# Layer 0 window attention: score matmuls of the two key groups issued in turns

## The chip, the cores and the metric

The kernel runs on 1 core of one Trainium2 chip, as one program. The metric is device time in microseconds (us). All numbers come from runs on the chip and from one profiled execution of the program before the change.

## What is computed

The reference is a two-layer trunk over 1024 tokens of 1024 features. Layer 0 runs two head groups side by side, windowed softmax attention with sinks and retention; layer 1 is a gated short convolution. Each layer then attends to 256 memory tokens, with norms before every part and plain residual sums. Only the windowed attention is touched here. Its 8 query heads share 2 key heads of 64 features, and the tokens are cut into 16 chunks of 64:

```python
g = A_Q_HEADS // A_KV_HEADS                       # 4 query heads for each key head
qc = q.reshape(b, n, CHUNK, A_KV_HEADS, g, d)     # CHUNK = 64, d = 64
kb, vb = band(k), band(v)                         # this chunk's and the two before: 192 keys
scores = jnp.einsum('bnqhgd,bnkhd->bnhgqk', qc, kb) * (d ** -0.5)
m = jnp.maximum(jnp.max(scores, axis=-1, keepdims=True), sink_logit)
p = jnp.exp(scores - m)
denom = jnp.sum(p, axis=-1, keepdims=True) + jnp.exp(sink_logit - m)
out = jnp.einsum('bnhgqk,bnkhd->bnqhgd', p / denom, vb)
```

## The kernel before

Every product of float32 values is made of three passes on TensorE: each operand is cut into a high and a low part, and `mm3` (lines 125 to 130) adds high x high (L128), high x low (L129) and low x high (L130) into one PSUM tile. Each matmul loads its stationary operand first; the profile shows these loads as PEld. The projections (`dense`) go into PSUM tiles named psd, 24 matmuls of 512 columns for each half of the tokens.

`even_layer` (line 409) makes the projections of keys, values and queries, then calls `window_chunk` for the 16 chunks; after every second chunk it calls `dense` for one of the eight gate projections. `window_chunk` does the following for chunk n. Keys lie with features on the partitions, the first key head in rows 0 to 63 and the second in rows 64 to 127, and so do the queries.

- The chunk's queries are split into qh and ql (ScalarE and VectorE, `split`, L144 and L145).
- Scores, in two groups g: rows 0 to 63 of the queries and keys, then rows 64 to 127. Each group takes a PSUM tile (pssc, a bank; two banks in all have this tag) and runs two `mm3`, one for each pair of query heads (jp): 64 rows deep, 128 queries, up to 192 keys. That is 6 matmuls for a group and 12 for a chunk. After each group VectorE reduces its tile to the maxima (mx, L283).
- nm and es (L287, L288), four exponentials on ScalarE (L290) that read the two pssc tiles, the sum, its reciprocal and four scalings on VectorE (L294 to L297) give the probabilities Pe (even chunks) or Po (odd chunks).
- TensorE transposes the probabilities (L311, tiles psa, 4 or 8 of 128 columns), they are split into Th and Tl, and two or four `mm3` multiply them with the values (psa). The results go back in place of the queries (Q, L324).

The order in which instructions stand on an engine is not that of the source. The program is scheduled when it is built: a scheduler with its own timing model takes ready instructions of all chunks and projections and writes one fixed order for each engine, with semaphore waits between engines. On TensorE the score matmuls of a chunk so stand among projection matmuls, value products and the transposes of an earlier chunk, in one stretch or in pieces.

The letters A and B below stand for the score matmuls of the first key group (rows 0 to 63) and of the second (rows 64 to 127); a run is a row of score matmuls on TensorE with no other matmul between them.

Of the kernel before, what the change touches and what calls it, by code (L numbers as in the profile page):

```python
# [19 lines left out]
PSUM = bass.MemoryType.PSUM  # L20
DRAM = bass.MemoryType.DRAM

P = 128
# [16 lines left out]
class Weights:  # L40
    """Streams [128, 1024] weight tiles: load, then an exact split into two float32r parts."""

# [35 lines left out]
class Trunk:  # L78
# [27 lines left out]

    # tiles: each tag is one stream of buffers
    BUFS = {"xh": 8, "xl": 8, "r": 8, "e": 4, "T": 5, "v": 4, "t": 5, "k": 4}
# [14 lines left out]

    # products
    def mm3(self, o, ah, al, bh, bl, first, last):
        """o += a.T @ b for a = ah + al, b = bh + bl, in three float32r passes."""
        mm = self.nc.tensor.matmul
        mm(o, ah, bh, start=first, stop=False)  # L128
        mm(o, ah, bl, start=False, stop=False)  # L129
        mm(o, al, bh, start=False, stop=last)  # L130

    def dense(self, xs, done, parts=((0, H), (H, S)), tags="d"):
        """One 128-feature tile of a projection, for each part of the tokens."""
        wh, wl = self.w.take()
        for i, (a, b) in enumerate(parts):
            ps = self.ps(tags if tags == "d" else tags[i])[:, : b - a]
            for kt in range(KT):
                c = slice(kt * P, kt * P + P)
                xh, xl = xs[kt]
                self.mm3(ps, wh[:, c], wl[:, c], xh[:, a:b], xl[:, a:b], kt == 0, kt == KT - 1)  # L140
            done(a, b, ps)
# [5 lines left out]
    def split_k(self, src, gain=None, two=False):  # L147
        """A [128, 1024] contraction tile's parts, times a gain."""
        nc = self.nc
        hi, lo = self.buf("xh", "xh", dt=F32R), self.buf("xl", "xl", dt=F32R)  # L150
        if gain is None:
            self.split(hi, lo, src)
        else:
            g = self.gains[:, gain : gain + 1]
            for c in halves(two):
                self.last_hi = nc.scalar.activation(hi[:, c], src[:, c], AF.Identity, scale=g)
                nc.vector.scalar_tensor_tensor(lo[:, c], src[:, c], g, hi[:, c].bitcast(F32),  # L157
                                               ALU.mult, ALU.subtract)
        return hi, lo

    def rsqrt(self, var, out=None):
        """(var + EPS) ** -0.5: exp(-ln/2), then a Newton step."""
        nc = self.nc
        n = var.shape[-1]
        r, t = self.buf("t", "rs", (P, n)), self.buf("t", "rt", (P, n))
        out = r if out is None else out
        nc.scalar.activation(r, var, AF.Ln, bias=self.eps)
        nc.scalar.activation(r, r, AF.Exp, scale=-0.5)
        self.last_act = nc.scalar.activation(t, r, AF.Square)
        nc.vector.scalar_tensor_tensor(t, var, EPS, t, ALU.add, ALU.mult)  # L170
        nc.vector.tensor_scalar(t, t, -0.5, 1.5, ALU.mult, ALU.add)
        nc.vector.tensor_tensor(out, t, r, op=ALU.mult)
        return out

    def use_set(self, name):
        """Load a set of activation functions, here in the Activation engine's program."""
        self.tc.keep_in_program_order(self.nc.scalar.preload_act_table_set(name))

    # norms
    def squares(self, m, x, sq, a, b, eng=None):  # L180
        """Square in place of sq, and add to the other features' sums."""
        nc = self.nc
        if m == 0:
            nc.scalar.activation(self.ssq[:, a:b], x, AF.Square)
        else:
            nc.scalar.activation(sq, x, AF.Square)  # L186
            if eng is not None:
                eng.tensor_tensor(self.ssq[:, a:b], self.ssq[:, a:b], sq, op=ALU.add)  # L188

    def mean(self, ones, sq):  # L190
        """The mean of [128, n] squares over the partitions, in each partition."""
        n = sq.shape[-1]
# [6 lines left out]
    def norm(self, rest):  # L199
        """R from the sums of squares and the rest's squares."""  # L200
        for c in (slice(0, H), slice(H, S)):
# [3 lines left out]
    def norm_soon(self, a, b, rest):  # L205
        """The same for tokens a to b, for when the tensor engine waits for it."""
        ps = self.ps("a")[:, : b - a]
# [4 lines left out]
    def scaled(self, out):  # L212
        """Evacuation that applies the tokens' norms; out: columns -> where to."""
        return lambda a, b, ps: self.nc.vector.tensor_tensor(out(a, b), ps, self.R[:, a:b],  # L214
                                                             op=ALU.mult)

    def out_proj(self, ys, x_old, x_new, between=iter(())):
        """x + y @ w, kept on chip and stored, and its squares."""
        nc = self.nc
# [17 lines left out]
    def last_proj(self, ys, x_old, parts):  # L237
        """x + y @ w and the last norm, one part of the tokens after the other."""
        nc = self.nc
# [19 lines left out]

    # layer 0: windowed attention with sinks  # L260
    def window_chunk(self, n, Q, Kh, Kl, V, Pt):
# [12 lines left out]
        mx, nm, sm, es = (self.small(k) for k in ("mx", "nm", "sm", "es"))  # L274
        sc = []
        for g in range(2):
            ps = self.ps("sc")
            r = slice(64 * g, 64 * g + 64)
            for jp in range(2):
                j = slice(jp * P, jp * P + P)  # L280
                self.mm3(ps[:, jp * 256 : jp * 256 + nk], qh[r, j], ql[r, j],
                         Kh[r, k0 : k0 + nk], Kl[r, k0 : k0 + nk], True, True)
            nc.vector.tensor_reduce(mx[:, 2 * g : 2 * g + 2],  # L283
                                    ps.rearrange("p (a b) -> p a b", a=2)[:, :, :nk],
                                    AX.X, ALU.max)
            sc.append(ps)
        nc.vector.scalar_tensor_tensor(nm, mx, -0.125, self.nsink, ALU.mult, ALU.min)  # L287
# [38 lines left out]
    def to_tokens(self, vt, name):  # L326
        """[128 features, tokens] -> [128 tokens, 8 x 128 features], split."""
        hi = self.buf("v", name + "h", dt=F32R)
# [9 lines left out]

    # layer 0: retention
    def rotated(self, t, cos, sin):  # L340
        """Rotary embedding in place, and its parts."""
        nc = self.nc
# [10 lines left out]
    def decayed_q(self, q, dec):  # L353
        """The second half's queries, decayed since the first half's end, split."""
        f, d = self.buf("t", "qd", (P, H)), self.buf("v", "qd", (P, 2, H), F32R)
# [4 lines left out]
    def decayed_k(self, k, h):  # L360
        """The first half's keys by token, decayed to the half's end, split."""
        nc = self.nc
# [45 lines left out]
    def even_layer(self, xs):  # L408
        """Both head groups; returns the output projection's contraction tiles and layer 0's
        memory keys and values."""  # L410
        nc, io = self.nc, self.io
# [64 lines left out]

    # layer 1: gated convolution
    def conv_in(self, xs, kv):
# [34 lines left out]

    # cross-attention
    def mem_norm(self):
        """The normed memory's split contraction tiles for both layers, kept in DRAM."""
        nc = self.nc
# [35 lines left out]
    def mem_k(self, mem):  # L553
        """Keys [features, keys] of the memory, split; one feature tile at each step."""
        K = [self.buf("e", "K", (P, KT, M), F32R) for _ in range(2)]
# [10 lines left out]
    def mem_v(self, mem):  # L566
        """Values [keys, features] of the memory, split; a quarter of the contraction for half
        of the features at each step."""
        V = [self.buf("e", "V", (P, 2, D), F32R) for _ in range(2)]
# [18 lines left out]
    def cross_unit(self, head, half, q, K, V, out):  # L588
        """Attention of one head's 512 tokens; out(dt, columns, PSUM) takes the values."""
        nc = self.nc  # L590
# [41 lines left out]
    def cross(self, xs, K, V):  # L632
        """The heads' values, as contraction tiles; those of all but the last head wait in place
        of the queries until the projections are done."""
        ys, wait = [], []
# [77 lines left out]
def _tiles(w):  # L713
    """[1024, n] -> [n / 128, 128, 8 * 128]: per feature tile, contiguous lines for each partition."""
    n = w.shape[1]
# [27 lines left out]
def _heads(w):  # L743
    """The last 512 columns' heads, as four tiles of [head j | head 4 + j]."""
    return w.reshape(w.shape[0], 2, 4, 64).transpose(0, 2, 1, 3).reshape(w.shape[0], 512)
# [65 lines left out]
```

## Time and profile before

| What | Value |
|---|---|
| time, median of 3 runs | 1514.37 us (1514.28 to 1515.32) |
| span of the profiled execution, first to last instruction | 1513.2 us |
| TensorE busy (matmuls) | 1483.5 us, 98% of the span, 7410 instructions |
| VectorE, ScalarE, GpSimd busy | 769.1, 564.8, 230.3 us |
| window attention with the gate projections | 78 to 226 us of the span |
| score matmuls in it | 192 of 849 matmuls |

The median lies 1.2 us above the span of the profiled execution; what a change does to the span is taken over to the median with that distance. Matmuls are pipelined: a matmul of 512 columns has a duration of 0.39 us in the trace while the next one starts 0.23 us later, so the distance between starts tells what one costs, and a row "x2" in the timeline merges neighbours of one kind.

### The profile page before, as it was taken

To read this page: it belongs to the slowest core of one execution; us is meant where nothing else is said; L and a number is where in the kernel's file an instruction comes from. 1 tells how busy PE (TensorE), PEld (TensorE's weight loads), DVE (VectorE), ACT (ScalarE), POOL (GpSimd) and SP (SyncE) were. 2 spreads that over 40 slices of the span, in tenths; PEclk is the share of its full clock that TensorE was granted. 3 is DMA by queue.
4 is the path that set the end of the run, shared out by engine and by line. 5 is a ranking of instruction groups with operands and counts; after the bars stand their busy time and mean duration, and the time that the engine had idled before them with its cause. 6 is when DMAs were issued, how large, how long until landed. Compare 5 with 4: busy or idle time off the path is not lost.

```text
span 1513.2 us, 18550 instructions
## 1 busy us (share of the span) xinstructions
PE 1483.5 (98%) x7410; PEld 1256.1 (83%) x7410; DVE 769.1 (51%) x1143; ACT 564.8 (37%) x983; POOL 230.3 (15%) x157
## 2 busy tenths in 40 slices
PE   8999999999999999999999999999999999999996
PEld 6878888888788888888888888888888888888996
DVE  7656765556673356444354333332336336446555
ACT  6434652433463244343243111211115225334554
POOL 2300103233401210000211111111110120000233
PEclk9999999999999999999999999999999999999998
DMA  5410104121464521002522221111123532111464
GB/s 212 165 44 29 56 29 139 58 82 43 139 209 153 167 82 44 29 29 70 193 81 102 63 63 56 56 56 56 42 84 113 180 127 74 36 30 40 133 206 151
DMA packets 44421, 140.77 MB, mean 93 GB/s; under 512 B 5552, under 2 KB 11824, under 8 KB 44080
## 3 DMA queue, kind: packets, MB, share of 16 engines
q1 hardware_dynamic: 44336, 139.60, 28.3%
q8 instruction: 58, 0.95, 0.3%
q14 instruction: 27, 0.22, 0.0%
HBM read 112.32 MB, written 23.07 MB: 89 GB/s over the span
## 4 chain that ended last, share of the span: by engine, by line
PE 85%; DVE 5%; DMA 4%; POOL 2%; ACT 1%; issue 1%; SPq 1%; DVEq 0%; POOLq 0%; ACTq 0%
PE psd L130 23%; PE psd L128 23%; PE psd L129 23%; PE pssc L130 3%; PE pssc L129 3%; PE pssc L128 3%; PE psa L128 2%; PE psa L129 2%; PE psa L130 2%; PE psa L311 1%; DMA swap<-bk 1%; DMA swap<-bq 1%; PE psa L621 1%; POOL bk L346 1%; POOL bq L346 1%
## 5 line engine op out<-in xcount | busy, mean ns | idle before, releaser
L128 PE MATMUL psd<-xh,whi 128*128 128x512 f32 (+2 forms) x1736 | 662.0, 384 | 8.4 <-ACT whi L64 7.3
L129 PE MATMUL psd<-xl,whi 128*128 128x512 f32 (+2 forms) x1736 | 663.9, 383 | 0.0
L130 PE MATMUL psd<-xh,wlo 128*128 128x512 f32 (+2 forms) x1736 | 663.1, 383 | 0.0
L128 PEld LDWEIGHTS psd<-xh,whi 128*128 128x128 f32 x1736 | 326.2, 188 | 69.5 <-ACT whi L64 7.8
L129 PEld LDWEIGHTS psd<-xl,whi 128*128 128x128 f32 x1736 | 326.3, 188 | 59.5 <-DVE xl L157 0.3
L130 PEld LDWEIGHTS psd<-xh,wlo 128*128 128x128 f32 x1736 | 326.2, 188 | 59.5
L64 ACT CAST whi<-wraw 128x1024 fp32r<-128x1024 f32 (+1 forms) x155 | 162.0, 1046 | 428.1 <-PE psd L129 306.7
L65 DVE TENSOR_TENSOR wlo<-wraw,whi 128x1024 fp32r<-128x1024 f32 (+1 forms) x155 | 200.6, 1295 | 68.0 <-ACT whi L64 66.1
L188 POOL TENSOR_TENSOR ssq<-ssq,xold 128x512 f32<-128x512 f32 (+2 forms) x54 | 78.1, 1446 | 573.6 <-ACT xold L186 484.3
L227 DVE TENSOR_TENSOR xnew<-psd,xold 128x512 f32<-128x512 f32 x48 | 32.9, 690 | 147.2 <-PE psd L130 143.8
L186 ACT ACTIVATE xold<-xnew 128x512 f32<-128x512 f32 (+2 forms) x63 | 36.4, 580 | 89.2 <-DVE xnew L227 48.9
L144 ACT CAST Th<-psa 128x512 fp32r<-128x512 f32 (+1 forms) x62 | 34.2, 588 | 68.9 <-PE psa L311 36.8
L145 DVE TENSOR_TENSOR Tl<-psa,Th 128x512 fp32r<-128x512 f32 (+1 forms) x62 | 42.1, 686 | 28.3 <-ACT Th L144 28.3
L488 POOL TENSOR_TENSOR y<-y,R 128x512 f32<-128x512 f32 x16 | 24.2, 1514 | 185.4 <-ACT y L487 185.4
L214 DVE TENSOR_TENSOR q<-psd,R 128x512 f32<-128x512 f32 x32 | 22.1, 691 | 53.9 <-PE psd L130 53.8
L611 ACT ACTIVATE P<-pssc,mx 128x256 f32<-128x256 f32 x64 | 29.5, 473 | 43.2 <-DVE mx L609 43.2
L214 DVE TENSOR_TENSOR z<-psd,R 128x512 f32<-128x512 f32 x16 | 11.1, 692 | 61.5 <-PE psd L130 61.5
L495 POOL TENSOR_TENSOR z<-z,R 128x512 f32<-128x512 f32 x16 | 20.7, 1295 | 132.6 <-DVE z L214 132.6
L491 DVE TENSOR_TENSOR y<-psd,y 128x512 f32<-128x512 f32 x16 | 11.0, 690 | 56.9 <-PE psd L130 56.9
L128 PE MATMUL psd<-mn,whi 128*128 128x256 f32 x128 | 36.8, 290 | 2.9 <-DVE K L145 2.9
L130 PE MATMUL psd<-mn,wlo 128*128 128x256 f32 x128 | 37.1, 290 | 0.8 <-DVE wlo L65 0.8
L498 DVE TENSOR_TENSOR z<-psd,z 128x512 f32<-128x512 f32 x16 | 11.1, 691 | 52.2 <-PE psd L130 52.2
(234 smaller groups left out, 1875.5 us busy)
## 6 DMA issues: line engine op xcount, KB each, us to landing
wraw<-w_o SPq DMA_DIRECT2D x32, 512.0 KB, 3.8
wraw<-w_o_in SPq DMA_DIRECT2D x32, 512.0 KB, 3.6
wraw<-w_e_in SPq DMA_DIRECT2D x25, 512.0 KB, 3.7
xold<-x SPq DMA_DIRECT2D x24, 512.0 KB, 4.7
x<-xnew SPq DMA_DIRECT2D x24, 512.0 KB, 2.6
wraw<-w_k SPq DMA_DIRECT2D x16, 512.0 KB, 3.8
wraw<-w_v SPq DMA_DIRECT2D x16, 512.0 KB, 3.6
wraw<-w_q SPq DMA_DIRECT2D x16, 512.0 KB, 3.6
```

Of the source, the lines that this page charges most:

```text
L64: self.nc.scalar.copy(hi[:, c], raw[:, c])
L65: self.nc.vector.tensor_tensor(lo[:, c], raw[:, c], hi[:, c].bitcast(F32), op=ALU.subtract)
L128: mm(o, ah, bh, start=first, stop=False)
L129: mm(o, ah, bl, start=False, stop=False)
L130: mm(o, al, bh, start=False, stop=last)
L144: self.nc.scalar.copy(hi, src)
L145: (eng or self.nc.vector).tensor_tensor(lo, src, hi.bitcast(F32), op=ALU.subtract)
L186: nc.scalar.activation(sq, x, AF.Square)
L188: eng.tensor_tensor(self.ssq[:, a:b], self.ssq[:, a:b], sq, op=ALU.add)
L214: return lambda a, b, ps: self.nc.vector.tensor_tensor(out(a, b), ps, self.R[:, a:b], op=ALU.mult)
L227: nc.vector.tensor_tensor(new[:, a:b], ps, old[:, a:b], op=ALU.add)
L346: nc.gpsimd.tensor_tensor(t, t, cos, op=ALU.mult)
```

## The change

In `window_chunk` both PSUM tiles are taken first. Then for each pair of query heads and each of the three passes the matmul of group 0 is followed by the matmul of group 1, and both reductions to the maxima come after all 12. The matmuls, their operands, their tiles and every other instruction are the same in kind and number. The diff also drops the docstrings and some comments of the file, which changes no instruction; source lines from 287 on stand one line later.

```diff
         mx, nm, sm, es = (self.small(k) for k in ("mx", "nm", "sm", "es"))
-        sc = []
-        for g in range(2):
-            ps = self.ps("sc")
-            r = slice(64 * g, 64 * g + 64)
-            for jp in range(2):
-                j = slice(jp * P, jp * P + P)
-                self.mm3(ps[:, jp * 256 : jp * 256 + nk], qh[r, j], ql[r, j],
-                         Kh[r, k0 : k0 + nk], Kl[r, k0 : k0 + nk], True, True)
+        sc = [self.ps("sc") for _ in range(2)]
+        rows = (slice(0, 64), slice(64, P))
+        keys = slice(k0, k0 + nk)
+        for jp in range(2):
+            j = slice(jp * P, jp * P + P)
+            for i, (a, b) in enumerate(((qh, Kh), (qh, Kl), (ql, Kh))):
+                for g, r in enumerate(rows):
+                    nc.tensor.matmul(sc[g][:, jp * 256 : jp * 256 + nk], a[r, j], b[r, keys],
+                                     start=i == 0, stop=i == 2)
+        for g, ps in enumerate(sc):
             nc.vector.tensor_reduce(mx[:, 2 * g : 2 * g + 2],
                                     ps.rearrange("p (a b) -> p a b", a=2)[:, :, :nk],
                                     AX.X, ALU.max)
-            sc.append(ps)
```

The scheduler writes another order from it, within the window stage alone: before the first score matmul and after the last chunk every engine's order is as it was. Chunk 9 on TensorE, before the change (pssc_1511 is A, pssc_1519 is B; the psa rows with ident are the transposes of chunk 8, psd is a gate projection):

```order
L128 MATMUL pssc_1511<-Kh_361,qh_1503 128x192
L311 MATMUL psa_1474<-ident,Pe_674 128x128 x4
L311 MATMUL psa_1481<-ident,Pe_674 128x128 x4
L129 MATMUL pssc_1511<-Kl_362,qh_1503 128x192
L130 MATMUL pssc_1511<-Kh_361,ql_1504 128x192
L128 MATMUL pssc_1511<-Kh_361,qh_1503 128x192
L129 MATMUL pssc_1511<-Kl_362,qh_1503 128x192
L130 MATMUL pssc_1511<-Kh_361,ql_1504 128x192
L128 MATMUL pssc_1519<-Kh_361,qh_1503 128x192
L129 MATMUL pssc_1519<-Kl_362,qh_1503 128x192
L130 MATMUL pssc_1519<-Kh_361,ql_1504 128x192
```

The same place after the change (pssc_1511 is A, pssc_1512 is B):

```order
L312 MATMUL psa_1474<-ident,Pe_674 128x128 x4
L312 MATMUL psa_1481<-ident,Pe_674 128x128 x4
L282 MATMUL pssc_1511<-Kh_361,qh_1503 128x192
L282 MATMUL pssc_1512<-Kh_361,qh_1503 128x192
L282 MATMUL pssc_1511<-Kl_362,qh_1503 128x192
L282 MATMUL pssc_1512<-Kl_362,qh_1503 128x192
L282 MATMUL pssc_1511<-Kh_361,ql_1504 128x192
L282 MATMUL pssc_1512<-Kh_361,ql_1504 128x192
L282 MATMUL pssc_1511<-Kh_361,qh_1503 128x192
L282 MATMUL pssc_1512<-Kh_361,qh_1503 128x192
L282 MATMUL pssc_1511<-Kl_362,qh_1503 128x192
L282 MATMUL pssc_1512<-Kl_362,qh_1503 128x192
```

The transposes, which stood behind the first A and cut the chunk's scores into runs of 1 and 11, now stand ahead of one run of 12, with A and B in turns.

Not every chunk stands so. Chunk 6 on TensorE after the change (pssc_1249 is A, pssc_1250 is B; psa with Th or Tl are value products of chunk 4):

```order
L282 MATMUL pssc_1249<-Kh_361,qh_1241 128x192
L282 MATMUL pssc_1249<-Kl_362,qh_1241 128x192
L282 MATMUL pssc_1249<-Kh_361,ql_1242 128x192
L128 MATMUL psa_1100<-Th_1084,Vh_424 128x256
L282 MATMUL pssc_1249<-Kh_361,qh_1241 128x192
L282 MATMUL pssc_1249<-Kl_362,qh_1241 128x192
L282 MATMUL pssc_1249<-Kh_361,ql_1242 128x192
L129 MATMUL psa_1100<-Tl_1085,Vh_424 128x256
L130 MATMUL psa_1100<-Th_1084,Vl_425 128x256
L128 MATMUL psa_1100<-Th_1084,Vh_424 128x256
L282 MATMUL pssc_1250<-Kh_361,qh_1241 128x192
L129 MATMUL psa_1100<-Tl_1085,Vh_424 128x256
```

Here value products went between the score matmuls, A and B do not stand in turns, and the chunk has four runs where it had three (AAAAAABBBB, B and B, with transposes between them).

Over the whole stage the program before has 36 runs: 20 with a transpose behind them and 16 with a projection matmul. The program after has 26 runs: 11 with a transpose behind them, 12 with a projection matmul and 3 with a value product. By chunk the runs are, with a comma between two runs of a chunk:

| chunk | before | after |
|---|---|---|
| 0 | AAAAAABBBBBB | ABABABABABAB |
| 1 | AAAAAAB, BBBBB | AAABBBAB, ABAB |
| 2 | AAAAAABB, B, BBB | AAAABBBBA, BAB |
| 3 | AAAAAABB, BBBB | AAAABBBBABAB |
| 4 | AAAAAABBBB, BB | ABABABABABAB |
| 5 | AA, AAAABBBBBB | AAAABBBBABAB |
| 6 | AAAAAABBBB, B, B | AAA, AAA, B, BBBBB |
| 7 | AA, AAAABBBBBB | AABBABABA, BAB |
| 8 | AAAAAABBBB, BB | AABBABABABAB |
| 9 | A, AAAAABBBBBB | ABABABABABAB |
| 10 | AAAAAABBBB, B, B | AAABBBABABA, B |
| 11 | AA, AAAABBBBBB | ABA, BABABABAB |
| 12 | AAAAAABBBB, B, B | AAABBBABABAB |
| 13 | AA, AAAABBBBBB | ABA, BABABABAB |
| 14 | AAAAAABBBB, B, B | AAABBBABABAB |
| 15 | A, AAAAABBBBBB | ABABA, BABABAB |

## Rows read from the trace of the kernel before

**Rows 1.** The page of the profile: the span, the busy time of four engines (share of the span, instructions), and the shares of the chain of work that ended last.

```profile
span 1513.2 us, 18550 instructions
PE 1483.5 (98%) x7410; PEld 1256.1 (83%) x7410; DVE 769.1 (51%) x1143; ACT 564.8 (37%) x983; POOL 230.3 (15%) x157
...
PE 85%; DVE 5%; DMA 4%; POOL 2%; ACT 1%; issue 1%; SPq 1%; DVEq 0%; POOLq 0%; ACTq 0%
```

**Rows 2.** Busy time of each engine by stretches of the span (number of instructions in brackets), then the granted TensorE clock as a share of 2.4 GHz, the share of the DMA engines and GB/s: the window stage, and four stretches behind it.

```profile
78.00:226.00 148.00, 148.00 (x849) 121.57 (x849) 93.52 (x248) 76.29 (x209) 4.60 (x1) 1.00 0.11 36
...
402.00:406.00 4.00, 1.49 (x9) 0.94 (x7) 2.88 (x3) 1.19 (x2) 2.31 (x2) 1.00 0.17 36
406.00:410.00 4.00, 3.89 (x15) 3.03 (x14) 4.00 (x7) 3.57 (x8) 0.06 (x1) 0.57 0.81 246
410.00:440.00 30.00, 26.89 (x207) 25.88 (x206) 23.39 (x32) 18.66 (x31) 7.64 (x6) 1.00 0.71 243
440.00:444.00 4.00, 3.62 (x17) 3.63 (x18) 3.51 (x7) 2.56 (x5) 0.00 (x0) 0.57 0.47 136
```

**Rows 3.** The chain of work that ended last, from 78 to 226 us, by line: shares of those 148 us.

```profile
by line: PE psd L129 20.9%; PE psd L128 20.8%; PE psd L130 20.7%; PE psa L311 10.3%; PE pssc L130 5.0%; PE pssc L128 5.0%; PE pssc L129 4.7%; PE psa L128 4.3%; PE psa L129 4.3%; PE psa L130 4.1%
```

**Rows 4.** TensorE's matmuls in order of time, chunk 8: start in us, duration in us, line, output and inputs, rows*columns of the array in use, moving operand.

```profile
152.27 0.35 PE L128 MATMUL pssc<-Kh,qh 64*128 64x192 f32 x1
152.46 0.27 PE L129 MATMUL pssc<-Kl,qh 64*128 64x192 f32 x1
152.57 0.27 PE L130 MATMUL pssc<-Kh,ql 64*128 64x192 f32 x1
152.58 0.38 PE L128 MATMUL pssc<-Kh,qh 64*128 64x192 f32 x2
152.78 0.29 PE L129 MATMUL pssc<-Kl,qh 64*128 64x192 f32 x2
152.89 0.29 PE L130 MATMUL pssc<-Kh,ql 64*128 64x192 f32 x2
153.00 0.27 PE L128 MATMUL pssc<-Kh,qh 64*128 64x192 f32 x1
```

**Rows 5.** The same view for the stationary loads of that run.

```profile
152.38 0.19 PEld L129 LDWEIGHTS pssc<-Kl,qh 64*128 64x128 f32 x1
152.49 0.19 PEld L130 LDWEIGHTS pssc<-Kh,ql 64*128 64x128 f32 x1
152.58 0.20 PEld L128 LDWEIGHTS pssc<-Kh,qh 64*128 64x128 f32 x2
152.69 0.21 PEld L129 LDWEIGHTS pssc<-Kl,qh 64*128 64x128 f32 x2
```

**Rows 6.** The chain of work that ended last, in order of time (start in us, us that the chain spent there): single score matmuls of chunk 10 among transposes and ahead of a projection.

```profile
172.45 0.81 PE psa L311 x6
173.25 0.28 PE pssc L129
173.54 0.37 PE psa L311 x2
173.90 0.28 PE pssc L130
174.19 0.43 PE psd L129
174.62 0.24 PE psd L130
```

**Rows 7.** The same view for the second run of chunk 5, AAAABBBBBB, with eight transposes ahead of it and a projection behind it.

```profile
125.00 1.02 PE psa L311 x8
126.03 0.28 PE pssc L130
126.31 0.11 PE pssc L128 x2
...
126.77 0.11 PE pssc L130
126.88 0.43 PE psd L129
```

**Rows 8.** The timelines of VectorE (the four scalings of the probabilities of a chunk) and of TensorE (the first transposes of the same chunk): chunk 9 (Po), then chunk 10 (Pe).

```profile
171.30 1.01 DVE L297 TENSOR_SCALAR Po<-Po,sm 128x192 f32<-128x192 f32 x4
...
172.38 0.66 PE L311 MATMUL psa<-ident,Po 128*128 128x128 f32 x4
...
180.62 1.01 DVE L297 TENSOR_SCALAR Pe<-Pe,sm 128x192 f32<-128x192 f32 x4
...
182.11 1.09 PE L311 MATMUL psa<-ident,Pe 128*128 128x128 f32 x8
```

**Rows 9.** TensorE's timeline in the last of those stretches: the first and the last of 14 matmuls of 256 columns, and two behind them.

```profile
440.75 0.41 PE L128 MATMUL psd<-mn,whi 128*128 128x256 f32 x1
...
443.53 0.40 PE L129 MATMUL psd<-mn,whi 128*128 128x256 f32 x1
443.74 0.31 PE L130 MATMUL psd<-mn,wlo 128*128 128x256 f32 x1
443.88 0.28 PE L128 MATMUL psd<-mn,whi 128*128 128x256 f32 x1
444.00 0.28 PE L129 MATMUL psd<-mn,whi 128*128 128x256 f32 x1
```

## Prediction

> **What bounds the kernel now.** I read the page first: TensorE is busy for 1483.5 of 1513.2 us, and 85% of the chain that ended last is its own [rows 1]. So a change helps if TensorE's own stream gets shorter, or if it waits less. Next I took the stage that the change touches. From 78 to 226 us TensorE is busy for all of the 148 us, the clock is granted at 1.00 (2.4 GHz), VectorE is busy for 93.52 us and ScalarE for 76.29 [rows 2]. The chain of this stage holds nothing but TensorE's lines: 14.7% of it is the score matmuls (three rows pssc, 5.0 + 5.0 + 4.7), or 21.8 us [rows 3]. The stage is bound by what TensorE's matmuls cost one after another, so I price the scores in that currency, distance between starts.
>
> **How a run of score matmuls is priced.** The timeline of chunk 8 shows three things [rows 4]. Within A the starts are 0.11 us apart (152.46, 152.57), which is also the distance of the loads of the stationary operand, 152.38 to 152.49 [rows 5]: a key group takes a matmul each 0.11 us, and I call that a slot. Second, A and B do run side by side already: at 152.58 two matmuls L128 are merged, the first B, 0.01 us behind the third A, and the fourth A at 152.69; from there on two matmuls and two loads come in each slot [rows 4, 5]. The first B stands four places behind the third A in the order, so a matmul can start once the one four places ahead has started. Third, work with other shapes costs extra. The first score matmul of a run takes 0.28 us of the chain where a further one takes 0.11 [rows 6, 7], so 0.17 for the way in. On the way out two transposes take 0.37 and eight 1.02 [rows 6, 7]; the difference of six is 0.65, or 0.108 each, so two are worth 0.22 and 0.15 is extra. A projection takes 0.43 instead of 0.24, so 0.20 with rounding [rows 6]. Each run thus has a fixed cost of 0.32 us with a transpose behind it, 0.37 with a projection, and 0.11 for each slot.
>
> Check on before: 20 x 0.32 + 16 x 0.37 = 12.3 us fixed. Slots by the rule: AAAAAABBBB is 6.8 (B begins 2.8 slots in), AAAABBBBBB is 6.2 (126.03 to 126.88 is 0.85 us, less 0.28 that is 5.2 slots behind the first, [rows 7]), a lone group its own number. Over the table of runs: 8.8 + 11 + 10 + 10 for chunks 0 to 3, 8.8 for each of the eight with AAAAAABBBB or A, AAAAABBBBBB, 8.2 for the four with AA, AAAABBBBBB: 143, times 0.11 is 15.7. Together 28.0 us. From the chain: 21.8 on the scores, and on the matmuls behind the runs 20 x 0.15 + 16 x 0.20 = 6.2, again 28.0.
>
> **The change part by part.** *Turns.* With A and B in turns each slot holds one of both from the start, so ABABABABABAB takes 6 slots. The scheduler does not give that everywhere; by the same rule the chunks 0 to 15 after take 6, 4+2, 5+2, 6.2, 6, 6.2, 3+3+1+5, 5+2, 6, 6, 6+1, 2+5, 6, 2+5, 6, 3+4: 108 slots. 143 - 108 = 35 slots, 3.8 us less. The bounds of this term: nothing at all, if A and B in turns run no better than the queue already lets them, and 47 slots or 5.2 us, if all 192 went in pairs (143 - 96).
>
> *Fewer runs.* 26 runs in place of 36, 11 with a transpose behind, 12 with a projection, 3 with a value product. The last kind has no row before; it lies between 0.32 and 0.37, and I take 0.37 since its stationary operand is loaded as a projection's is. 11 x 0.32 + 15 x 0.37 = 9.1 us, 3.2 less than 12.3. This follows from the order alone and doesn't depend on pairs.
>
> *What else moves.* The number of matmuls, of DMAs and of all other instructions is the same, and nothing moves outside the stage, so SP's and GpSimd's queues see the same rows. Both reductions now come behind the twelfth matmul, where the first was done under B's matmuls. What hides that is the distance from the scalings to the transposes of the chunk: in chunk 9, the narrowest, the scalings end at 172.31 and TensorE starts the transposes at 172.38; in chunk 10, the next, they end at 181.63 and the transposes start at 182.11 [rows 8]. In chunk 9 0.07 us is left, and I count 0.1 us of waiting for it; in the others 0.5 us or more covers the later reduction, and it costs nothing. Both PSUM banks must be free when a chunk's scores begin, where A's alone had to be; the exponentials that free them end before the scalings do, so this wait is the smaller one, and I count nothing. Bounds of the two: 0, and 1.6 us if each of the 16 chunks lost 0.1.
>
> Sum: 3.8 + 3.2 - 0.1 = 6.9 us of TensorE's stream. The stages behind it start that much earlier; they are driven by TensorE's own progress and keep their length. Span 1506.3, and with the distance of 1.2 us between span and median, 1507.5 us.
>
> A rule of the Trainium skill says otherwise on the pairs. The rows show B's first matmul running beside A's third and ahead of A's fourth to sixth, which stand earlier in the order [rows 4]. TensorE: Matmul & The Clock Gate, section Part 3: Packing small matmuls, says that matmuls start and end strictly in program order. By that rule before would hold 192 slots and the 36 runs would cost 12.3 + 21.1 = 33.4 us, where the chain shows 28.0; the turns would then save up to 10.6 us instead of 3.8. The trace does not agree, and I go by the rows.
>
> **The rivals.** *The supply is too slow.* No row shows more than two matmuls a slot over four slots, and there only one place of the order had to be brought in for each slot, since A and B were drawn from two places of it. With full turns two have to be. If TensorE's sequencer brings one matmul with its load in 0.11 us, five are at hand at the start and a run of n takes n - 4 slots: 8 in place of 6 for a run of twelve, and over the nine runs of eleven or twelve 17 slots or 1.8 us more: 1509.3 us. Chance 0.14. (The Trainium skill, TensorE: Matmul & The Clock Gate, section Wait — 56ns, not 53.3ns?, gives about 62 ns for each matmul where firmware decodes it; by it twelve matmuls need 0.74 us and not 0.66, an estimate of 0.7 us over the nine runs, so 1508.2 us. No run here shows which decoding is at work.)
>
> *Turns bring nothing, only the fewer runs do.* Then 3.2 us remain, 1514.4 - 3.1 = 1511.3. Against it stands that a B in its own bank beside an A is seen in the rows [rows 4, 7]. This is also the case in which the change does not do what it says. Chance 0.05.
>
> *New waits.* TensorE comes to transposes or scores earlier than VectorE and ScalarE deliver, because the order of these two engines changed as well. For it: 0.07 us of cover in chunk 9 [rows 8]. Against it: the two are busy 63% and 52% of the stage [rows 2]. With 0.2 us in each chunk 3.2 us are lost: 1510.6. Chance 0.07.
>
> *Slower: each change of key group exposes its load.* At the head of a run the second A starts 0.19 us behind the first [rows 4]. If every change between A and B cost that, 192 x 0.19 = 36.5 us, with the fixed 9.1 us 45.6 instead of 28.0: 1532 us. It decides from 0.098 us a matmul on, (28.0 - 9.1) / 192, where the rows show 0.055 with A and B alternating for four slots. Chance 0.05.
>
> *Strict order.* If A and B did not overlap before and do after, the turns would be worth up to 96 x 0.11 = 10.6 us, with the fewer runs 13.8: 1500.6 us. The check of 28.0 us speaks against it. Chance 0.01. (It is what the page's rule on program order would give.)
>
> **How the numbers follow.** The forecast, within about 1 us, has 0.68. Predicted 1507.5. Besides the cases, the clock adds a spread of its own: behind the stage it is granted at 0.57 on average in two stretches of 4 us, 406 to 410 and 440 to 444, each behind a stretch in which TensorE had stood idle for 2.5 us or more [rows 2]; one of them gone or one more is about 1.3 us by the second, where 14 matmuls started 0.21 us apart and the next ones 0.12 [rows 9]. With the slow supply below and the better bound of the turns above, 1505.5 to 1510.8 leaves out the cases at 1511.3 and 1532, part of the waits and the strict order: some 0.15. A measurement of this kernel can tell about 0.2%, 3.0 us, from no change. Faster by more than that: forecast, slow supply, strict order, most of the waits and half of the case at 1511.3, 0.88. Within: 0.07. Slower: 0.05.
>
> **What would show it.** In the profile after: score rows as x2 pairs from the head of a run, starts 0.11 us apart for a pair; the stage from 78 us ending near 219 in place of 226; the chain of the stage with about 10% for the scores; no idle time of TensorE in it. Starts of 0.19 us within a run would show the exposed load, gaps ahead of L312 the late probabilities, pairs that fall apart after the second slot the slow supply. Wrong altogether would be the pricing, if the stage got shorter by 7 us while the score runs kept their lengths.

## The result and the profile after

The changed kernel takes 1507.99 us (median of four runs, 1506.56 to 1509.92) beside 1514.84 us of the kernel before (1514.28 to 1518.75, four runs). The ratio is 0.9948, with a 95% interval of 0.9932 to 0.9964 (5.5 to 10.3 us): 6.9 us less at the median, where 6.9 were forecast. A second comparison (the last experiment below) gives 0.9966, 0.9953 to 0.9978.

The page of the kernel after, the lines that answer to [rows 1]: TensorE's busy time fell by 7.0 us and the span by 6.4.

```profile
span 1506.8 us, 18553 instructions
...
PE 1476.5 (98%) x7410; PEld 1251.4 (83%) x7410; DVE 769.5 (51%) x1143; ACT 564.3 (37%) x983; POOL 230.4 (15%) x157
...
PE 87%; DVE 4%; DMA 4%; POOL 2%; ACT 1%; issue 1%; SPq 0%; DVEq 0%; POOLq 0%; ACTq 0%
```

Windows of the kernel after: the stage, and two stretches behind it (columns as in [rows 2]).

```profile
78.00:219.00 141.00, 140.95 (x849) 116.88 (x848) 93.23 (x248) 74.50 (x202) 4.62 (x1) 1.00 0.12 39
396.00:400.00 4.00, 1.08 (x5) 0.56 (x3) 2.33 (x2) 0.62 (x1) 3.24 (x2) 1.00 0.00 0
400.00:404.00 4.00, 3.53 (x15) 3.37 (x16) 4.00 (x7) 3.61 (x8) 0.00 (x0) 0.57 0.84 249
```

As many matmuls, 849, as filled 148 us now fill 141, and TensorE is idle for 0.05 us of them. The chain of the stage, by line, answers to [rows 3]: the scores (now one line, L282) are 11.6% of 141 us, 16.4 us, where they were 21.8. The prediction said about 10%; its own prices (26 times 0.17 for the way in and 108 slots) make 16.3 us.

```profile
by line: PE psd L128 22.0%; PE psd L130 21.5%; PE psd L129 21.4%; PE pssc L282 11.6%; PE psa L312 9.8%; PE psa L129 4.8%; PE psa L128 4.6%; PE psa L130 4.4%; issue 0.0%
```

How it looks in one run, to be set beside [rows 4]: TensorE's timeline of the kernel after, eleven score matmuls of chunk 10 (AAABBBABABA) between a projection and the transposes of chunk 9.

```profile
167.84 0.40 PE L130 MATMUL psd<-xh,wlo 128*128 128x512 f32 x1
168.17 0.36 PE L282 MATMUL pssc<-Kh,qh 64*128 64x192 f32 x2
168.36 0.28 PE L282 MATMUL pssc<-Kl,qh 64*128 64x192 f32 x2
...
168.69 0.28 PE L282 MATMUL pssc<-Kl,qh 64*128 64x192 f32 x2
168.81 0.27 PE L282 MATMUL pssc<-Kh,ql 64*128 64x192 f32 x1
169.12 0.73 PE L312 MATMUL psa<-ident,Po 128*128 128x128 f32 x5
```

Every row but the odd last one is a pair (x2) from the head of the run, 0.11 us behind the one before; only the first slot takes 0.19. Five pairs and one single are six slots. Chunk 9, twelve in full turns between transposes and a projection, is six pairs:

```profile
161.07 0.36 PE L282 MATMUL pssc<-Kh,qh 64*128 64x192 f32 x2
...
161.71 0.28 PE L282 MATMUL pssc<-Kh,ql 64*128 64x192 f32 x2
```

No pair falls apart, so the sequencer brings two matmuls a slot.

For the experiments I need one number for each kernel, the cost of its score runs: for each run, the time from the start of the last matmul ahead of it to the start of the second matmul behind it, less what these two take among their own kind (a projection 0.228 us, a value product 0.119, a transpose 0.109). It is taken from the trace and summed over all runs; where a single matmul stands between two runs, its interval is counted once. The stage I measure from the start of the first score matmul to the end of the last value product: from 80.41 to 239.55 before, 159.14 us, and from 81.41 to 233.76 after, 152.35 us, 6.8 less. What comes behind it took 1273.61 us before (1513.16 - 239.55) and 1273.07 after (1506.83 - 233.76).

### The profile page after: what moved, and what is told of

Same layout as the page of the kernel before. It is cut to its first block, busy times and chain, and to the rows that moved or that the text cites. A ratio compares the mean times of both kernels' runs of the same rounds, so it can differ in the third digit from the quotient of the medians.

```text
span 1506.8 us, 18553 instructions
## 1 busy us (share of the span) xinstructions
PE 1476.5 (98%) x7410; PEld 1251.4 (83%) x7410; DVE 769.5 (51%) x1143; ACT 564.3 (37%) x983; POOL 230.4 (15%) x157
## 4 chain that ended last, share of the span: by engine, by line
PE 87%; DVE 4%; DMA 4%; POOL 2%; ACT 1%; issue 1%; SPq 0%; DVEq 0%; POOLq 0%; ACTq 0%
PE psd L128 23%; PE psd L130 23%; PE psd L129 23%; PE pssc L130 3%; PE pssc L129 2%; PE pssc L128 2%; PE psa L129 2%; PE psa L128 2%; PE psa L130 2%; DMA swap<-bk 1%; PE pssc L282 1%; DMA swap<-bq 1%; PE psa L312 1%; PE psa L622 1%; POOL bk L347 1%
## 5 line engine op out<-in xcount | busy, mean ns | idle before, releaser
L496 POOL TENSOR_TENSOR z<-z,R 128x512 f32<-128x512 f32 x16 | 20.7, 1296 | 132.6 <-DVE z L214 132.6
```

## The experiments

The theory under test is the prediction's pricing: each run of score matmuls has a fixed price (0.32 us with a transpose behind it, 0.37 otherwise), each slot costs 0.11, and how many slots a run needs follows from the order by the rule of four places ahead. The rivals are that only the runs count, that only the turns count, that two run together only where they stand next to each other in the order, and that the gain came from the order of the other engines.

**The turns taken out, the rest left in.** A's six first, then B's; both banks still taken first, both reductions still behind the twelfth matmul.

```diff
-        for jp in range(2):
-            j = slice(jp * P, jp * P + P)
-            for i, (a, b) in enumerate(((qh, Kh), (qh, Kl), (ql, Kh))):
-                for g, r in enumerate(rows):
...
+        for g in range(2):
+            r = slice(64 * g, 64 * g + 64)
+            for jp in range(2):
+                j = slice(jp * P, jp * P + P)
+                self.mm3(sc[g][:, jp * 256 : jp * 256 + nk], qh[r, j], ql[r, j],
+                         Kh[r, k0 : k0 + nk], Kl[r, k0 : k0 + nk], True, True)
```

> The change without the turns: both PSUM banks are taken first and both reductions stand behind the twelfth matmul, but all six matmuls of A come ahead of the six of B. TensorE's order then holds the 36 runs of the kernel before, matmul for matmul. Theory (the gain comes from what TensorE's order holds, 0.32 or 0.37 us a run and 0.11 us a slot): 28.0 us for the scores as before, no difference, 1514.5 us. Rival (the gain comes from the later reductions and the earlier taking of the second bank, by another order on VectorE and ScalarE): most of the 6.9 us, about 1508. A new wait from the later reductions would show as up to 1.6 us above the kernel before.

Measured: 1515.49 us beside 1515.72, ratio 1.0001 (0.9992 to 1.0009). The runs cost 27.9 us and the stage takes 159.14 us, as before to the hundredth. The later reductions and the earlier taking of the second bank do nothing in either direction; and without the turns the scheduler makes the old 36 runs again. Both terms of the sum, the slots and the fewer runs, thus come through the order of the matmuls.

**Fewer runs without turns.** The chunk's function is cut in two (scores and softmax; transposes and value products), the next chunk's first part is traced ahead of this chunk's second part, and two constraints hold each chunk's scores together between the value products and the transposes.

```diff
+        part = self.window_chunk(0, Q, Kh, Kl, V, Pt)
         for n in range(16):
-            self.window_chunk(n, Q, Kh, Kl, V, Pt)
+            this = part
+            if n < 15:
+                part = self.window_chunk(n + 1, Q, Kh, Kl, V, Pt)
+            self.window_values(n, *this, V, self.last_score)
...
+        with self.tc.issue_after(self.last_value.ins) if n > 1 else nullcontext():
+            for g in range(2):
...
+            with self.tc.issue_after(after.ins):
+                for c in range(4):
+                    nc.tensor.transpose(ps[:rows, c * P : c * P + P],
```

> Blocks AAAAAABBBBBB again, but each chunk's scores are held together and put between the value products and the transposes, so that there are 16 runs in place of 36, 15 with a transpose behind and one with a projection. Theory: fixed 15 x 0.32 + 0.37 = 5.2 us, slots 16 x 8.8 = 141 or 15.5 us, together 20.7, 7.3 us less than before: 1507.2 us, although no turns are in it. Rival (only the pairs count, a run has no price of its own): 143 slots become 141, 0.2 us less, 1514.3. Either can lose up to 3 us where a chunk's transposes now stand only some 8 us behind its scores and VectorE's scalings end 5 to 9 us behind them in the changed kernel; that would show as idle time ahead of L312's counterpart, and the cost of a run is then read from the trace.

Measured: 1507.58 us, ratio 0.9950 (0.9936 to 0.9963), 7.6 us less at the ratio. The runs cost 20.5 us (20.7 expected). So a run has a price of its own, and the rival by which only pairs count (1514.3) is out. TensorE's timeline of this kernel, one run of twelve between value products and transposes:

```profile
130.97 0.28 PE L132 MATMUL psa<-Th,Vl 128*128 128x256 f32 x1
131.18 0.35 PE L130 MATMUL pssc<-Kh,qh 64*128 64x192 f32 x1
131.38 0.27 PE L131 MATMUL pssc<-Kl,qh 64*128 64x192 f32 x1
131.49 0.27 PE L132 MATMUL pssc<-Kh,ql 64*128 64x192 f32 x1
131.50 0.37 PE L130 MATMUL pssc<-Kh,qh 64*128 64x192 f32 x2
131.69 0.29 PE L131 MATMUL pssc<-Kl,qh 64*128 64x192 f32 x2
131.80 0.29 PE L132 MATMUL pssc<-Kh,ql 64*128 64x192 f32 x2
131.91 0.27 PE L130 MATMUL pssc<-Kh,qh 64*128 64x192 f32 x1
132.03 0.27 PE L131 MATMUL pssc<-Kl,qh 64*128 64x192 f32 x1
132.14 0.27 PE L132 MATMUL pssc<-Kh,ql 64*128 64x192 f32 x1
```

B's first matmul, the seventh in the order, starts at 131.50 with A's third, four places ahead of it; pairs last until A is through, and B's last three run alone. The transposes begin at 132.34, 1.16 us behind the head of the run.

**The turns added to that.** The same kernel with the change's loops, A and B in turns.

```diff
-            for g in range(2):
-                r = slice(64 * g, 64 * g + 64)
-                for jp in range(2):
...
+            for jp in range(2):
+                j = slice(jp * P, jp * P + P)
+                for i, (a, b) in enumerate(((qh, Kh), (qh, Kl), (ql, Kh))):
+                    for g, r in enumerate(rows):
...
```

> As e2, with ABABABABABAB in each of the 16 runs (one has AAABBBABABAB). Theory: fixed 5.2 us, slots 97 or 10.6 us, together 15.8, 12.2 us less than before and 4.9 less than e2: 1502.3 us, and a run of twelve of 0.98 us against 1.29 in e2. Rival (turns bring nothing): the time of e2, 1507.2. Rival (only pairs count): 143 - 97 = 46 slots, 5.1 us less than before, 1509.4. The wait ahead of the transposes named for e2 would here be up to 0.3 us a chunk larger, as the runs are shorter: up to 1507 where it takes all of it.

Measured: 1502.51 us, ratio 0.9915 (0.9901 to 0.9928). This kernel has the lowest median of the study, below both the kernel before and the change. The runs cost 15.6 us (15.8 expected), 4.9 less than in blocks. Its timeline, the run that answers to the one above:

```profile
129.76 0.28 PE L132 MATMUL psa<-Th,Vl 128*128 128x256 f32 x1
129.97 0.36 PE L285 MATMUL pssc<-Kh,qh 64*128 64x192 f32 x2
130.16 0.27 PE L285 MATMUL pssc<-Kl,qh 64*128 64x192 f32 x2
...
130.61 0.27 PE L285 MATMUL pssc<-Kh,ql 64*128 64x192 f32 x2
130.81 0.98 PE L321 MATMUL psa<-ident,Po 128*128 128x128 f32 x7
```

Six pairs, and the transposes 0.84 us behind the head: 0.32 us or three slots less than in blocks. Here a slot saved is a slot of the stage: neither the transposes nor the banks are waited for. The stage is 14.2 us shorter than before, 1.6 us of which are seven projection matmuls (412 in place of 419, 0.228 us each) that now come behind it; the stretch behind it is 2.0 us longer.

**In threes.** The same 16 runs with AAABBBAAABBB.

```diff
+            for jp in range(2):
+                j = slice(jp * P, jp * P + P)
+                for g in range(2):
+                    r = slice(64 * g, 64 * g + 64)
+                    self.mm3(sc[g][:, jp * 256 : jp * 256 + nk], qh[r, j], ql[r, j],
+                             Kh[r, k0 : k0 + nk], Kl[r, k0 : k0 + nk], True, True)
```

> As e2, with AAABBBAAABBB in each run. Theory (a matmul can start once the one four places ahead has started, so a block of three of one group hides the next block of the other): 6.1 slots a run, 98 in all, as e3 within 0.2 us a kernel: 1502.4, runs of 0.98 to 1.00 us. Rival (two run together only where A and B stand next to each other in the order, so at the three borders of a run): 12 - 3 = 9 slots, 144, 15.8 us, the time of e2, runs of 1.30 us.

Measured: 1504.24 us, ratio 0.9923 (0.9911 to 0.9936). That interval overlaps the one of the turns, so the two times can't be told apart. The cost of the runs decides about the rival: 15.7 us, beside 15.6 with full turns, where the rival asked for 21.0 (5.2 fixed + 15.8). The timeline shows why:

```profile
131.77 0.36 PE L130 MATMUL pssc<-Kh,qh 64*128 64x192 f32 x2
131.97 0.28 PE L131 MATMUL pssc<-Kl,qh 64*128 64x192 f32 x2
...
132.62 0.98 PE L320 MATMUL psa<-ident,Po 128*128 128x128 f32 x7
```

The first row is a pair at once: B's first, the fourth in the order, starts with A's first, ahead of A's second and third. So full turns aren't needed; blocks of three are as good.

**In threes, with the scheduler free.** The change's own form with the loops just shown, and no constraint on where the scores stand.

> The change with its twelve matmuls written in threes, AAABBBAAABBB, and nothing held in place: the scheduler makes 31 runs of it, 15 with a transpose behind and 16 with a projection, and by the rule of four places ahead they hold 127 slots (six where a run is AAABBBAA, as many as the table of the order gives elsewhere). Theory: 15 x 0.32 + 16 x 0.37 + 127 x 0.11 = 24.7 us, 3.3 less than before: with before at 1515.5 that is 1512.2. Rival (two run together only where A and B stand next to each other in the order): about 12 - 2 slots for a chunk in two runs, 160 slots, 28.3 us, no gain: 1515.8. Rival (only pairs have a price, runs have none): 16 slots, 1.8 us less, 1513.7.

Measured: 1511.70 us, ratio 0.9977 (0.9969 to 0.9986), beside 1514.90: 3.2 us less, 3.3 expected. The runs cost 24.4 us (24.7 expected), the stage takes 155.71 us. Both rivals, at 1513.7 and 1515.8 us, lie outside the interval (1510.2 to 1512.8 us). This is the sharpest test of the sum with both terms in it, since neither the number of runs nor that of slots is that of another kernel.

**Turns in many runs.** Each chunk's second half of the scores is held behind the transposes of the chunk before.

```diff
+        yield
+        with self.tc.issue_after(self.last_tr.ins) if n > 0 else nullcontext():
+            j = slice(1 * P, 1 * P + P)
+            for i, (a, b) in enumerate(((qh, Kh), (qh, Kl), (ql, Kh))):
```

> As e3, with the turns, but the second half of each chunk's scores (jp = 1) is held behind the transposes of the chunk before, so that there are 37 runs of 3 to 12 matmuls, all with a projection behind. Theory: 37 x 0.37 + 117 slots x 0.11 = 13.7 + 12.9 = 26.6 us, 11 more than e3 though every matmul is still written in turns: 1.4 less than before, 1514.1 with before at 1515.5. Rival (the turns give e3 its gain, the runs little): 117 slots against 97, 2.2 us above e3, 1504.7.

Measured: 1522.78 us, ratio 1.0054 (1.0040 to 1.0068), 8 us slower than before, where 1.4 less was expected. The price of the runs held: the 37 runs cost 27.6 us, of which 1.2 come on top of the price in one place, the run of 190 to 193 us, where two matmuls wait for the exponentials that free their banks; the rest is 26.4, and 26.6 were expected.

```profile
191.66 0.35 PE L282 MATMUL pssc<-Kh,qh 64*128 64x192 f32 x1 [0.34 <-ACT Po L300]
191.86 0.27 PE L282 MATMUL pssc<-Kl,qh 64*128 64x192 f32 x1
192.47 0.36 PE L282 MATMUL pssc<-Kh,qh 64*128 64x192 f32 x1 [0.34 <-ACT Po L300]
```

So by the scores it stands where the kernel before does (27.9), and the rival by which the turns alone give the gain (1504.7) is out. The 8 us came from what was left out of the expectation: held in two pieces, the chunks are spread over more projections (537 projection matmuls in the stage in place of 419), the stage ends at 268 us in place of 240, and the next stage's work comes to TensorE before it is ready. The timeline at 270 and at 412 us, and two windows:

```profile
270.39 0.39 PE L132 MATMUL psd<-xh,wlo 128*128 128x512 f32 x1
273.81 0.63 PE L383 MATMUL psa<-ident,bk 128*128 128x128 f32 x4 [3.03 <-DVE bk L366]
...
274.92 0.61 PE L130 MATMUL psd<-xh,whi 128*128 128x512 f32 x1
275.33 0.63 PE L131 MATMUL psd<-xl,whi 128*128 128x512 f32 x1
...
412.14 1.09 PE L383 MATMUL psa<-ident,bk 128*128 128x128 f32 x4 [2.99 <-DVE rs L423]
```

```profile
276.00:278.00 2.00, 2.00 (x6) 1.52 (x6) 2.00 (x1) 0.92 (x2) 2.00 (x1) 0.50 0.04 8
...
410.00:450.00 40.00, 33.00 (x224) 31.52 (x225) 28.59 (x42) 24.56 (x44) 8.91 (x8) 0.86 0.61 204
```

TensorE stands for 3.03 us, and soon after it goes at half the clock, with projections 0.42 us apart in place of 0.23. It stands for another 2.99 us before 412; from 410 to 450 the granted clock is 0.86, where the kernel before has 0.96 over the same stretch. Over the whole span TensorE is busy 4.0 us longer than before (1487.5 against 1483.5) and idle 4.4 us longer (34.1 against 29.7). Which order of which engine makes bk late was not tried, so that the spreading is the cause is argued from these rows and not shown by a run.

**No work on 64 rows at all.** Each group's stationary operand has zeros in the other group's half, and the matmul runs over all 128 rows.

```diff
-        qh = self.buf("k", "qh", (P, 256), F32R)
+        qh = self.buf("k", "qh", (P, 2, 256), F32R)
+                nc.gpsimd.memset(q[z, g, :].bitcast(F32), 0.0)
...
-                        self.last_score = nc.tensor.matmul(sc[g][:, jp * 256 : jp * 256 + nk], a[r, j], b[r, keys],
+                        self.last_score = nc.tensor.matmul(sc[g][:, jp * 256 : jp * 256 + nk], a[:, g, j], b[:, keys],
```

> As e3, but each key group's stationary operand is a tile of 128 rows with zeros in the other group's half, so that all 192 score matmuls use 128 rows, as transposes and projections do, and none can run beside another; the output is the same sums. It adds small splits on ScalarE and VectorE and 64 fills of zeros on GpSimd, and one buffer of another stage is left out for room. Theory A (the fixed price of a run is that of going between work on 64 rows and work on 128): 192 x 0.11 = 21.1 us and nothing fixed, against 15.5 measured in e3: 5.6 above e3, 1508.1, with the first score matmul of a run 0.11 us apart from its neighbours. Theory B (the fixed price belongs to the scores for another reason, such as their bank or their operands): 21.1 + 16 x 0.32, 10.8 above e3, 1513.3.

Measured: 1510.44 us, ratio 0.9969 (0.9957 to 0.9981). The time alone lies between the two theories, 2.3 us above A and 2.9 below B; the trace decides. First the timeline, then the chain of one run:

```profile
125.90 0.28 PE L132 MATMUL psa<-Th,Vl 128*128 128x256 f32 x1
126.02 0.37 PE L289 MATMUL pssc<-Kh,qh 128*128 128x192 f32 x2
126.23 0.38 PE L289 MATMUL pssc<-Kl,qh 128*128 128x192 f32 x2
...
127.12 0.39 PE L289 MATMUL pssc<-Kh,ql 128*128 128x192 f32 x2
127.34 0.71 PE L325 MATMUL psa<-ident,Pe 128*128 128x128 f32 x5
```

```profile
126.18 1.32 PE pssc L289 x12
127.51 0.33 PE psa L325 x3
```

The first score matmul starts 0.12 us behind the value product, where it is 0.21 in the 64-row kernels above; the first transpose stands 0.11 behind the last score matmul (two in 127.12 to 127.34), where it is 0.20; three transposes take 0.33. Twelve matmuls at 0.11 and nothing else: the fixed price belongs to the going to and fro between work on 64 and on 128 rows.

Chunk 2 shows the same within one kernel, without the added splits and fills. The value products ahead of its scores are those of chunk 0, which has 64 keys, and so they use 64 rows. In the kernel before the scores behind them pay no way in; in this kernel, at 128 rows, they do, and in this chunk alone. TensorE's timelines there, before and in this kernel:

```profile
96.84 0.28 PE L130 MATMUL psa<-Th,Vl 64*128 64x256 f32 x1
96.96 0.25 PE L128 MATMUL pssc<-Kh,qh 64*128 64x192 f32 x1
97.05 0.27 PE L129 MATMUL pssc<-Kl,qh 64*128 64x192 f32 x1
```

```profile
99.11 0.28 PE L132 MATMUL psa<-Th,Vl 64*128 64x256 f32 x1
99.31 0.36 PE L289 MATMUL pssc<-Kh,qh 128*128 128x192 f32 x1
99.51 0.27 PE L289 MATMUL pssc<-Kl,qh 128*128 128x192 f32 x1
```

Before, the run AAAAAABB of chunk 2 costs 0.79 us and the run AAAAAABB of chunk 3, behind value products on 128 rows, 0.99; with zeros the run of twelve of chunk 2 costs 1.52 and most others 1.32 to 1.33. So theory B is out by the traces of both kernels.

All runs cost 21.8 us; beyond the price of 21.1, 0.2 are this way in of chunk 2 and some 0.4 are waits in two other chunks. The time above theory A is only in part accounted for. The stage has a wait of 0.43 us for the split of the probabilities of chunk 8, and what comes behind it takes 2.7 us more than before (1276.30 against 1273.61), which I haven't followed up. The profiled execution is also the slowest of the six, 3.2 us above their median, with its first score matmul at 81.85 us where the kernel before has it at 80.41.

**The change once more.**

> The changed kernel once more, beside the same runs of the kernel before: 6.9 us less by the prediction, 1508.6 with before at 1515.5. If the small spread at the kernel's opening (a wait of about 1 us at 9 us in the profiled run) is in some executions alone, the times spread from about 1506.5 to 1510.

Measured: 1508.44 us (1507.96 to 1511.93, so one time above the spread that was expected) beside 1514.90, ratio 0.9966 (0.9953 to 0.9978). The stage takes 152.34 us, as in the first profile (152.35). What differs is the opening, where the first profile shows a wait that this execution hasn't; its first score matmul starts at 80.73 and not at 81.41. TensorE's timeline of the first profile:

```profile
8.59 1.05 PE L130 MATMUL psd<-xh,wlo 128*128 128x512 f32 x2
10.35 0.79 PE L128 MATMUL psd<-xh,whi 128*128 128x512 f32 x1 [0.71 <-ACT xh L156]
```

All kernels side by side; the price is runs times 0.32 or 0.37 plus slots times 0.11, as expected ahead of each run, the cost is that of the trace:

| kernel | runs | slots | price, us | cost in the trace, us | ratio to before |
|---|---|---|---|---|---|
| blocks, scheduler free (order of before) | 36 | 143 | 28.0 | 27.9 | 1.0001 |
| threes, scheduler free | 31 | 127 | 24.7 | 24.4 | 0.9977 |
| the change | 26 | 108 | 21.0 | 21.0 | 0.9948, 0.9966 |
| blocks in 16 runs | 16 | 141 | 20.7 | 20.5 | 0.9950 |
| threes in 16 runs | 16 | 98 | 15.9 | 15.7 | 0.9923 |
| turns in 16 runs | 16 | 97 | 15.8 | 15.6 | 0.9915 |
| turns in 37 runs | 37 | 117 | 26.6 | 27.6 | 1.0054 |
| all on 128 rows, 16 runs | 16 | 192 | 21.1 | 21.8 | 0.9969 |

## Why the prediction was right

*The bound.* It stood: the stage is TensorE's own stream before and after, busy for 140.95 of 141 us, and what the runs lose in cost (27.9 - 21.0 = 6.9 us) the stage loses in length (159.14 - 152.35 = 6.8) and the median in time (6.9). That the median agrees with the forecast to a tenth is luck, since its interval is 5.5 to 10.3 us wide and the second comparison gave 6.5; the cost of the runs in the trace is the firm reading.

*The turns, 3.8 us.* The slots were right. The clearest reading is the pair of kernels with 16 runs, which differ in nothing but the turns: 44 slots by the rule, 4.8 us by the price, 4.9 in the trace. The rule of four places, read from one row of the kernel before, held for blocks, threes and turns alike. By TensorE: Matmul & The Clock Gate (the Trainium skill, section Part 3: Packing small matmuls) matmuls start strictly in program order, which would leave nine slots in a run AAABBBAAABBB; the trace shows six and B's first ahead of A's second, so it does not agree. The prediction's sum by that rule, 192 slots before, is too high by 16: where B follows A, A's last and B's first can share a slot in strict order too. That makes 176 slots and 31.7 us in place of 33.4, still well above the 28.0 of the chain.

*Fewer runs, 3.2 us.* Right too: 36 runs against 16, both in blocks, cost 7.4 us more in the trace, where the prices give 7.3. What the prediction could not say was where the price comes from; the kernel with 128 rows throughout and chunk 2 show it. TensorEngine Tiling (the Trainium skill, section Key Properties) says that a change of the tiling mode drains TensorE. It gives no time for it; here it is 0.32 us for going in and out, and nothing where no run changes the mode. The one price that had no row before, a value product behind a run, is the 0.37 taken: the three such runs, all in chunk 6 (three, three and one matmul of one group), cost 1.87 us together, and less seven slots (0.77) that is 0.37 each.

*The waits, 0.1 us.* As priced. VectorE's scalings of chunk 9 and chunk 10 in the kernel after, to be set beside [rows 8]:

```profile
168.66 1.01 DVE L298 TENSOR_SCALAR Po<-Po,sm 128x192 f32<-128x192 f32 x4
...
177.85 1.01 DVE L298 TENSOR_SCALAR Pe<-Pe,sm 128x192 f32<-128x192 f32 x4
```

In chunk 9 they end at 169.67, and the first transposes start at 169.12: TensorE takes each probability tile as it comes. The run of eleven ahead of them (chunk 10's) costs 1.08 us, where the full runs of chunks 8, 12 and 14 cost 0.99 to 1.00: some 0.09 us of waiting, in the place that was named. In chunk 10 the transposes start at 178.59 with the scalings through at 178.86; the cover of 0.5 us is gone there too, at no visible cost.

*The rivals.* The slow supply would have given runs of eight slots; every run of twelve in turns has six. The full runs of 0.99 us, less 0.32, leave 0.67 us for twelve matmuls, so the 0.74 of the estimate in that rival is out too. Turns that bring nothing, and changes of group that expose their load, are refuted by the same rows. The order of the other engines, which no rival of the prediction named as a source of gain, is excluded by the blocks with the scheduler free.

*Behind the stage.* Said to keep its length: 1273.61 us before, 1273.07 and 1273.09 after. Inside it things did move: in the first profile one stretch at 0.57 of the clock is left (400 to 404, again behind a stretch with TensorE busy for 1.08 of 4 us) where [rows 2] have two. In the kernels with 16 runs on 64 rows the stretch is 1.7 to 2.4 us longer, and the projections that stand behind the stage there and not in it (five to seven at 0.228 us) are 1.1 to 1.6 of it.

## What to carry to other kernels

Count the places where TensorE goes from work on part of its rows to work on all of them, and price them, before counting matmuls: here a round trip costs as much as three slots, and putting each chunk's scores into one run gained as much as the change did, without any turns. Two row groups needn't alternate one by one; it is enough that a matmul of the other group stands within four places. And read what a scheduler makes of a new order: nearly half of this change's gain (3.2 of 7.0 us by the prices) came from ten runs fewer, which its lines don't mention, while a constraint that spread the same work differently lost 8 us in a later stage.

## What the runs showed of the hardware that was not expected

A matmul on other rows starts ahead of earlier ones in the order: in blocks the seventh at 131.50 us with the third, in threes the fourth with the first, ahead of the second and third. Going from 128 rows to 64 and back costs 0.32 us (0.21 in place of 0.12 on the way in, the first slot 0.19 in place of 0.11, 0.20 in place of 0.11 ahead of the first transpose, and in the trace 0.17 in place of 0.11 ahead of the second); with zeros in the other half, at 128 rows throughout, it is gone, and scores behind a value product that itself uses 64 rows pay no way in. And in the kernel with 37 runs a stand of 3.03 us of TensorE at 270 us was followed by projections 0.42 us apart in place of 0.23, at a granted clock of 0.50 (1.2 GHz), so that this wait cost more than its own length.
